# A gated up projection by Strassen's block product for 38 of 44 column pairs, with the up and the down projection as two phases

## The chip, the cores and the metric

The kernel runs on one core of a Trainium2 chip. The metric is device time in microseconds of one execution. The kernel before takes 2750.92 us, the median of three runs (2749.88 to 2751.28).

## The reference

One layer of a hybrid encoder block for 16 meta tokens followed by 512 tokens of width 2048, in float32. What bears on the change is its second half:

```
r = r + rmsnorm(mixer(rmsnorm(r)))
h = rmsnorm(r, ffn_pre_g)                       # 2048 features
a = causal_dwconv(h @ w_up, conv_w, conv_b)     # 2048 -> 2 x 5632, width 3 along the tokens
gate, val = split(a, 2)
r = r + rmsnorm((gelu_tanh(gate) * val) @ w_down, ffn_post_g)   # 5632 -> 2048
return r[:, 16:]
```

The mixer ahead of it (forgetting attention and multi-scale pools, their gates, then W_out) ends in 16 feature tiles `m` of 128 features, which W_out multiplies.

## The kernel before

Activations lie transposed, 128 features by tokens; weights are the stationary operand of TensorE (PE). Each float32 product is carried as three: x_hi*w_hi, x_lo*w_hi, x_hi*w_lo, where hi is the value rounded to the float32r multiplier's 12 bits and lo = value - hi. So one 128x128 weight tile and one block of tokens take three matmuls. Past the mixer only 514 tokens count (two meta tokens, since the convolution looks two back), in two halves: 258 and 256 columns.

**Weights.** `order` lists chunks of 16 weight tiles. Each chunk moves in two halves of 128x1024 (`load_next`, L133, on SP's DMA queue, six buffers). `convert_next` makes hi by a copy on ScalarE (ACT, L146) and lo by a subtraction on VectorE (DVE, L147), into four buffers each. `weights` calls it one to two halves ahead of the matmuls that use them.

**Side work.** `Side` holds Python generators that emit work for ACT, DVE, POOL and SP between the matmuls. `tick` counts the matmuls' columns at 2330 columns per us; when the time that a generator yielded has run out, its next piece is emitted. Only the first generator of the list runs. `finish` emits all that is left at once. Every engine then executes its instructions in the order in which they were emitted, and waits at an instruction whose operands or buffer aren't ready.

**Order around the change.** W_out runs for 16 output tiles; some for both halves of the tokens, the others first for half 0 and then for half 1. Beside its last 12 steps (half 1) runs `mixer_norm` of half 0: residual, second RMSNorm, and hi and lo of h (L701 to L718). The norm's factor per token (`rs2`) is left out of h and multiplied in when the product of W_up leaves PSUM (L759, L774). Then the first five gate/value pairs of W_up run in halves (`up_half`): all ten tiles for half 0, beside `mixer_norm` of half 1, then all ten for half 1, beside `combine`. The other 39 pairs run whole (`up_full`, L770): 16 weight tiles x 3 x 2 halves = 96 matmuls for a gate tile and 96 for a value tile. `combine` (L738 to L746) does the convolution, the gelu and the product with the value, and splits the result into hi and lo.

W_up and W_down alternate: `up_group(g+1)` makes four pairs, `down` multiplies the four tiles of group g with W_down and adds to 16 accumulators in SBUF (L806, L808). The last group of W_down runs in two halves of the tokens with the last norm beside it (`final`).

SBUF holds 68 slots of 128x528 float32 for activations (`F`). PSUM has three tiles of two banks and two tiles of one bank.

Of the kernel before, what the change touches and what calls it, by code (L numbers as in the profile page):

```python
# [23 lines left out]
RAW, HI, LO = 6, 4, 4  # L24
NOUT = 6
# [11 lines left out]
HB = T0 + NA  # L37
H = 8
# [4 lines left out]
EPS = 1e-6  # L43
NEG = -1e30
# [16 lines left out]
def block(ctx, tc, xT, win, wf, wao, wpw, wpo, wout, wup, wdn, consts, out):  # L61
# [5 lines left out]
    fp = ctx.enter_context(tc.tile_pool(name="act", bufs=68))  # L67
    wp = ctx.enter_context(tc.tile_pool(name="wts", bufs=2))
    sp = ctx.enter_context(tc.tile_pool(name="small", bufs=4))
    pp = ctx.enter_context(tc.tile_pool(name="psum", bufs=2, space=PSUM))  # L70
# [8 lines left out]
    def s_ps(name):  # L79
        return pp.tile([P, 512], F32, name=name, tag="s", bufs=2)  # L80
# [25 lines left out]
    # W_out: some tiles for all tokens at once, the others for each half of the tokens  # L106
# [15 lines left out]
    # each chunk holds 16 tiles of [128, 128] and moves in two halves  # L122
    raws, ready = [], []
    at = {"load": 0, "conv": 0, "use": 0}
    NL = 2 * len(order)

    def load_next():
        n = at["load"]
        if n < NL:
            key = order[n // 2]  # L130
            raw = wp.tile([P, 1024], F32, name="wraw", tag="wraw", bufs=RAW)
            c = 1024 * (n % 2)
            nc.sync.dma_start(raw, srcs[key[0]](*key[1:])[:, c:c + 1024])  # L133
            raws.append(raw)
            at["load"] += 1

    def convert_next(copy=act.copy):
        n = at["conv"]
        if n < NL - 8:
            if n == at["load"]:  # L140
                load_next()
            raw = raws[n]
            raws[n] = None
# [4 lines left out]
            ready.append((hi, lo))  # L148
            at["conv"] += 1

    def weights(*key, ahead=1):
        """the next chunk, as a function from the tile's number to its hi and lo parts"""
# [3 lines left out]
        while at["conv"] < min(NL - 8, 2 * n + 2 + (2 if ahead else -1)):  # L156
            convert_next()
        while at["load"] < min(NL, 2 * n + 2 + 2 * ahead + RAW):
            load_next()
        def w(t):  # L160
            if t >= 8 and ahead:
                while at["conv"] < min(NL - 8, 2 * n + 5):
                    convert_next()
            c = P * (t % 8)
            hi, lo = ready[2 * n + t // 8]
            return hi[:, c:c + P], lo[:, c:c + P]
        return w

    def last_weights(i):
        """tile i of the last group of W_down, in slots of the activations"""  # L170
        at["quarter"] = at.get("quarter", 2 * NL - 2 * 4 * 2)
        while at["quarter"] < min(2 * NL, 2 * NL - 16 + i + 5):
            q = at["quarter"]
            raw = raws[q // 2][:, 512 * (q % 2):512 * (q % 2 + 1)]
# [4 lines left out]
            while at["load"] < min(NL, q // 2 + 1 + RAW):  # L179
                load_next()  # L180
# [5 lines left out]
    class Side:  # L186
        """generators, one after another, that emit work and yield how long (us of products) to wait"""
# [27 lines left out]
    def mm3(parts, nk, w, x):  # L215
        """parts: (psum slice, rhs slice); w(k), x(k) -> (hi, lo)."""
        us = sum(3 * (xs.stop - xs.start) / 2330.0 for _, xs in parts)
        for k in range(nk):
            wh, wl = w(k)
            xh, xl = x(k)  # L220
            for j, (a, b) in enumerate(((wh, xh), (wh, xl), (wl, xh))):
                for po, xs in parts:
                    pe.matmul(po, a, b[:, xs], start=k == 0 and j == 0, stop=k == nk - 1 and j == 2)  # L223
            side.tick(us)

# [6 lines left out]
    def rstd_from(accs, dst, n, ps=None):  # L232
        """dst = 1 / sqrt(sum over the partitions and accs / D + EPS), on every partition"""
# [97 lines left out]
    def forget():  # L331
        """c = cumsum(logsigmoid(f))"""
# [88 lines left out]
    def attention(h, r):  # L421
# [5 lines left out]
        # values: [keys, head dim]  # L427
# [11 lines left out]
        # scores of the two meta queries the convolution reaches back to  # L439
# [35 lines left out]
        # P^T: [keys, queries]  # L475
# [83 lines left out]
    def half_proj(name, w, i, xs_h, xs_l):  # L559
        """an M-tile of a product with K = 1024; weights hold two M-tiles."""  # L560
# [3 lines left out]

    mp, sig = [], {}
    for i in range(16 + LAG):
        if i < 16:
            sig[i] = gate("pga", 32 + i)
        if i >= LAG:
# [8 lines left out]
            mp.append(m)  # L578

# [39 lines left out]
    HALF = [(0, NA, T0), (NA, NB, HB)]  # L619
    mh, ml = [None] * KT, [None] * KT  # L620

    def split_m(e, ks):
        o, n, c = HALF[e]
        for k in ks:
            if e == 0:
                mh[k], ml[k] = F("mh", F32R), F("ml", F32R)
            split(mp[k][:, c:c + n], mh[k][:, c:c + n], ml[k][:, c:c + n])

    for i in range(16 + LAG2):
        if i < 16:  # L630
# [14 lines left out]
        if i >= 16:  # L645
            split_m(0, range(14) if i == 16 else (14, 15))

# [7 lines left out]
    r_dram = dp.tile([KT, P, SEQ], F32, name="r_dram")  # L655
    hb = [[], []]
    rs2 = rstd[:, T0:]
# [4 lines left out]
    def mixer_out(i, es):  # L662
        w = weights("out", i)
        if len(es) == 2:
            big = mm_ps("pw2")
            pss = [big[:, 254:512], big[:, 512:768]]
        else:
            pss = [s_ps("pw")[:, :HALF[es[0]][1]]]
        mm3([(ps, slice(HALF[e][2], HALF[e][2] + HALF[e][1])) for e, ps in zip(es, pss)], KT, w,
            lambda k: (mh[k], ml[k]))  # L670
        for e, ps in zip(es, pss):
            n = HALF[e][1]
            t = mix[e][i] = F("mix", n=NA)
            act.copy(t[:, :n], ps)
            sq = F("sq2", n=NA)
            act.activation(sq[:, :n], ps, AF.Square)  # L676
            if macc[e] is None:
                macc[e] = sq
            else:
                dve.tensor_tensor(macc[e][:, :n], macc[e][:, :n], sq[:, :n], op=OP.add)  # L680

    def mixer_norm(e, mix, acc, pace):
        o, n, c = HALF[e]
        yield 4.0
        rs1, acc2 = F("rs1", n=NA), F("acc3", n=NA)
        xs = [None] * (KT + 3)

        def x_load(i):
            if i < KT:
                xs[i] = F("x2", n=NA)  # L690
                nc.sync.dma_start(xs[i][:, :n], xT[i][:, c:c + n])
# [3 lines left out]
        rstd_from([acc], rs1[:, :n], n)  # L695
        rows = []
        for i in range(KT + 2):
            yield pace
            if i < KT:
                t = mix[i]  # L700
                dve.scalar_tensor_tensor(t[:, :n], t[:, :n], col(C_G[1] + i), rs1[:, :n], op0=OP.mult, op1=OP.mult)  # L701
            if i >= 2:
                p, hl, g, sq = rows[i - 2]
                dve.scalar_tensor_tensor(hl[:, NA:NA + n], p[:, :n], g, f32(hl[:, :n]), op0=OP.mult, op1=OP.subtract)
                if i > 2:
                    pool.tensor_tensor(acc2[:, :n], acc2[:, :n], sq[:, :n], op=OP.add)
                rows[i - 2] = None
            if i < KT:
                pool.tensor_tensor(t[:, :n], t[:, :n], xs[i][:, :n], op=OP.add)
                xs[i] = None  # L710
                x_load(i + 3)
                rows.append((t, F("h2", F32R, 516), col(C_G[2] + i), F("sq3", n=NA) if i else acc2))
                s = max(c, META)
                nc.sync.dma_start(r_dram[i][:, s - META:c + n - META], t[:, s - c:n])
            if 1 <= i <= KT:
                p, hl, g, sq = rows[i - 1]
                act.activation(hl[:, :n], p[:, :n], AF.Identity, scale=g)
                act.activation(sq[:, :n], p[:, :n], AF.Square)  # L718
                hb[e].append(hl)
        yield 3.0  # L720
        rstd_from([acc2], rs2[:, o:o + n], n)
# [10 lines left out]
    yacc = [None] * KT  # L732

    def combine(zg, zv, f, acts):
# [16 lines left out]
        yield 0.1  # L751

    def up_half(e, m, z):
        o, n, c = HALF[e]
        w = weights("up", m)
        ps = s_ps("pu0")
        mm3([(ps[:, :n], slice(0, n))], KT, w,
            lambda k: (hb[e][k][:, :n], hb[e][k][:, NA:NA + n]))
        dve.tensor_tensor(z[:, o:o + n], ps[:, :n], rs2[:, o:o + n], op=OP.mult)  # L759

    def up_full(m):
        w = weights("up", m)
        ps = mm_ps("pup")
# [180 lines left out]
```

## Time and profile before

| what | value |
|---|---|
| time, median of 3 runs | 2750.92 us (2749.88 to 2751.28) |
| profiled execution, span from the first to the last instruction | 2750.2 us |
| PE busy | 2701.5 us, 98% of the span, 20581 matmuls |
| DVE busy | 1332.0 us, 48% |
| ACT busy | 872.1 us, 32% |
| POOL busy | 146.1 us, 5% |
| mean granted TensorE clock | 0.993 of full |
| moved by DMA | 289.87 MB, mean 105 GB/s |

The page gives the span of the profiled execution and no other time for it; it lies 0.7 us below the median of the runs. Busy shares are means over stages that differ. Matmuls are pipelined (one lasts about 0.28 us while the next starts 0.12 us after it), so that PE's rate is read from the distances between starts.

### The profile page before, as it was taken

The numbers are of one execution on the slowest core, as the hardware profiler recorded it, in microseconds if no ns is written. First come the engines' busy times: TensorE is split into PE (matmuls) and PEld (weight loads), VectorE is DVE, ScalarE is ACT, GpSimd is POOL, SyncE is SP. The second block draws the span as 40 slices with busy tenths as digits, with TensorE's granted clock in tenths as the row PEclk, the third lists the DMA queues.
The fourth block names the chain that finished last, engine by engine and source line by source line (L and its number), as shares of the span: only waits on it lengthen the run. The fifth ranks groups of instructions, "written<-read, shape, count | busy, mean of one in ns | idle before, by whom it ended". The sixth has DMA issues, their size and how long they took to land. (4 is left out here: it accounts for less than half of the span.)

```text
span 2750.2 us, 47156 instructions
## 1 busy us (share of the span) xinstructions
PE 2701.5 (98%) x20581; PEld 2604.2 (95%) x20581; DVE 1332.0 (48%) x1762; ACT 872.1 (32%) x1214; POOL 146.1 (5%) x176
## 2 busy tenths in 40 slices
PE   8999999999999999999999999999999999999996
PEld 7999999999999999999989898989898989898985
DVE  7655543223533344687633545353535444444447
ACT  4433342222322233555432222222222222222223
POOL 3000000000000000143000000000000000000003
PEclk9999999999999999999999999999999999999998
DMA  4322222222222224676422222222222222222223
GB/s 175 101 86 78 74 81 95 95 94 88 92 92 93 93 92 131 200 223 209 142 94 93 92 93 94 95 96 93 92 93 96 93 96 92 93 92 94 91 77 123
DMA packets 93967, 289.87 MB, mean 105 GB/s; under 512 B 10294, under 2 KB 26936, under 8 KB 93760
## 3 DMA queue, kind: packets, MB, share of 16 engines
q1 hardware_dynamic: 93056, 284.68, 31.0%
q8 instruction: 161, 2.64, 0.4%
q0 software_dynamic: 704, 2.18, 0.3%
q14 instruction: 46, 0.38, 0.0%
HBM read 278.41 MB, written 8.41 MB: 104 GB/s over the span
## 5 line engine op out<-in xcount | busy, mean ns | idle before, releaser
L147 DVE TENSOR_TENSOR wlo<-wraw,whi 128x1024 fp32r<-128x1024 f32 x494 | 613.9, 1245 | 581.8 <-ACT whi L146 578.0
L146 ACT CAST whi<-wraw 128x1024 fp32r<-128x1024 f32 x494 | 516.3, 1048 | 1174.3 <-PE pup L770 445.8
L770 PE MATMUL pup<-h,whi 128*128 128x258 f32 (+1 forms) x4992 | 794.5, 281 | 0.0
L770 PEld LDWEIGHTS pup<-h,whi 128*128 128x128 f32 x4992 | 681.3, 189 | 0.8
L770 PE MATMUL pup<-h,wlo 128*128 128x258 f32 x2496 | 501.1, 282 | 0.0
L770 PEld LDWEIGHTS pup<-h,wlo 128*128 128x128 f32 x2496 | 382.5, 189 | 0.0
L774 DVE TENSOR_TENSOR z<-pup,rstd 128x514 f32<-128x514 f32 x78 | 54.1, 694 | 262.6 <-PE pup L770 262.6
L223 PE MATMUL pw<-mh,whi 128*128 128x258 f32 (+1 forms) x512 | 135.0, 284 | 3.8 <-ACT sq L676 3.7
L223 PE MATMUL pw<-mh,wlo 128*128 128x258 f32 (+1 forms) x512 | 134.6, 283 | 0.0
L223 PE MATMUL pw<-ml,whi 128*128 128x258 f32 (+1 forms) x512 | 134.4, 283 | 0.0
L223 PE MATMUL pdm<-fl,whi 128*128 128x512 f32 x320 | 126.1, 394 | 0.0
L223 PE MATMUL pdm<-fh,wlo 128*128 128x512 f32 x320 | 126.0, 394 | 0.0
L223 PE MATMUL pd<-fh,whi 128*128 128x512 f32 x320 | 125.9, 393 | 0.0
L223 PE MATMUL pdm<-fh,whi 128*128 128x512 f32 x320 | 125.9, 393 | 0.0
L223 PE MATMUL pd<-fl,whi 128*128 128x512 f32 x320 | 125.7, 393 | 0.0
L223 PE MATMUL pd<-fh,wlo 128*128 128x512 f32 x320 | 125.7, 393 | 0.0
L223 PE MATMUL pu<-h,whi 128*128 128x258 f32 (+1 forms) x640 | 118.5, 288 | 1.8 <-DVE z L759 1.8
L808 DVE TENSOR_TENSOR yacc<-yacc,pd 128x512 f32<-128x512 f32 x72 | 49.5, 687 | 125.4 <-PE pd L223 125.4
L223 PEld LDWEIGHTS pu<-h,whi 128*128 128x128 f32 x640 | 101.1, 194 | 2.1 <-issue 2.0
L223 PE MATMUL pga<-xh,whi 128*128 128x258 f32 (+1 forms) x512 | 102.8, 282 | 0.0
L223 PE MATMUL pgp<-xh,wlo 128*128 128x258 f32 (+1 forms) x512 | 102.5, 282 | 0.0
L223 PE MATMUL pga<-xh,wlo 128*128 128x258 f32 (+1 forms) x512 | 102.4, 281 | 0.0
(294 smaller groups left out, 4857.8 us busy)
## 6 DMA issues: line engine op xcount, KB each, us to landing
wraw<-wup SPq DMA_DIRECT2D x196, 512.0 KB, 3.5
wraw<-win SPq DMA_DIRECT2D x128, 512.0 KB, 3.5
wraw<-wdn SPq DMA_DIRECT2D x88, 512.0 KB, 3.4
wraw<-wout SPq DMA_DIRECT2D x56, 512.0 KB, 3.6
wraw<-wao SPq DMA_DIRECT2D x16, 512.0 KB, 3.4
wraw<-wpo SPq DMA_DIRECT2D x16, 512.0 KB, 3.6
xr<-xT SPq DMA_DIRECT2D x16, 264.0 KB, 6.2
r_dram<-mix SPq DMA_DIRECT2D x32, 128.0 KB, 2.8
```

Of the source, the lines that this page charges most:

```text
L146: copy(hi, raw)
L147: dve.tensor_tensor(lo, raw, f32(hi), op=OP.subtract)
L223: pe.matmul(po, a, b[:, xs], start=k == 0 and j == 0, stop=k == nk - 1 and j == 2)
L770: pe.matmul(ps[:, 254 + o:254 + o + n], a, hb[e][k][:, b:b + n], start=k == 0 and j == 0, stop=k == KT - 1 and j == 2)
L774: dve.tensor_tensor(z[:, :NT], ps[:, 254:768], rs2, op=OP.mult)
L808: dve.tensor_tensor(yacc[i], yacc[i], ps, op=OP.add)
```

## The change

It takes the same result by another order of sums. For 38 of the 44 pairs, W_up's two tiles (gate, value) by its two halves of the input features form a 2x2 block matrix A, and h by feature halves and token halves a 2x2 block matrix B. Instead of eight block products the kernel takes seven (Winograd's form of Strassen's product): A11*B11, A12*B21, S2*T2, S1*T1, S3*T3, A22*B22 and S4*T4, where S1 = A21+A22, S2 = S1-A11, S3 = A11-A21, S4 = A12-S2, and T1 to T4 are such sums of blocks of h. Each block product is 8 weight tiles x 3 matmuls of 258 columns; both token halves have 258 columns and share two.

- The weight stream is now a list of loads and a list of conversions (`units`). A pair loads four halves and converts seven; the four sums of weights are made by DVE in `unit_source`. `pair_weights` converts three units ahead (LOOK).
- `up_pair` runs the seven products into three PSUM banks a, b, c. Some add onto a bank that already holds a product (`more`), after a copy of it (`snap`, ACT) has been taken for another output. Three sums on DVE and one copy on ACT make the gate and the value.
- The sums of h need the finished norm: `mixer_norm` now makes two passes per half, first residual and squares, then h with its factor, its hi and lo, and a copy of h to DRAM. `sums_of_h` loads the copies and makes T1 to T4 with hi and lo, beside the second half of the pairs in halves, of which there are now six; there `combine` is put ahead of it in the list.
- All of W_up runs before W_down. `combine` writes the gated tile to DRAM (GpSimd's DMA queue); `act_group` loads four tiles and splits them.
- There are 62 slots in place of 68. Ten of the mixer's 16 tiles `m` go through DRAM between its stages (`mp_store`, `mp_load`). From the FFN on PSUM is eight tiles of one bank. `final` loads the residual in smaller steps.

```diff
-    NH = 5
+    NH = 6
     ups = lambda f0, f1: [("up", s * FT + f) for f in range(f0, f1) for s in (0, 1)]
     order += ups(0, NH) * 2
-    for g in range(NG):
-        if g + 1 < NG:
-            order += ups(max(NH, (g + 1) * GRP), (g + 2) * GRP)
-        order += [("dn", g, m) for m in range(4)]
+    order += [("pair", f) for f in range(NH, FT)]
+    order += [("dn", g, m) for g in range(NG) for m in range(4)]
...
+            units += [(i, at0) for i in ("11", "12", "S2", "S1", "S3", "S4", "22")]
...
+        if kind == "S3":
+            def done():
+                drop(n + 2)
+                dve.tensor_tensor(a12, a12, sums["s2"], op=OP.subtract)
+            return a21, done
+        if kind == "S4":
+            return a12, lambda: drop(n + 1)
+        if kind == "S1":
+            def done():
+                dve.tensor_tensor(a21, a11, a21, op=OP.subtract)
+                drop(n)
+            return sums["s1"], done
...
+        dve.tensor_tensor(s1, a21, a22, op=OP.add)
+        dve.tensor_tensor(s2, s1, a11, op=OP.subtract)
+        return s2, lambda: None
...
+        def unit(i):
+            prepare(u + i + 1 + LOOK)
+            load_ahead()
...
-    def mixer_norm(e, mix, acc, pace):
+    def mixer_norm(e, mix, acc, pace, pace2):
...
+            if i > 2:
+                (dve if i % 2 else pool).tensor_tensor(acc2, acc2, sqs[i - 2], op=OP.add)
...
+        yield 2.0
+        rstd_from([acc2], rs2, n)
+        for i in range(KT + 1):
+            yield pace2
+            if i:
+                hl = hb[e][i - 1]
+                dve.tensor_tensor(hl[:, NA:], mix[i - 1], f32(hl[:, :NA]), op=OP.subtract)
+            if i < KT:
+                t = mix[i]
+                dve.scalar_tensor_tensor(t, t, col(C_G[2] + i), rs2, op0=OP.mult, op1=OP.mult)
+                hl = F("h2", F32R, 2 * NA)
+                act.copy(hl[:, :NA], t)
+                nc.sync.dma_start(h_dram[e, i], t)
                 hb[e].append(hl)
...
-            side.add(mixer_norm(0, mix[0], macc[0], 2.7))
+            side.add(mixer_norm(0, mix[0], macc[0], 2.2, 2.0))
     side.finish()
-    side.add(mixer_norm(1, mix[1], macc[1], 2.1))
+    side.add(mixer_norm(1, mix[1], macc[1], 1.8, 1.5))
...
+    def sums_of_h():
+
+        for k in range(HK):
+            t13, t24 = F("t13", n=2 * NA), F("t24", n=2 * NA)
+            for t, parts in ((t13, ((0, k), (1, k))), (t24, ((1, HK + k), (0, HK + k)))):
+                for j, (e, i) in enumerate(parts):
+                    nc.sync.dma_start(t[:, NA * j:NA * (j + 1)], h_dram[e, i])
+            yield 4.0
+            b11, b12, b22, b21 = t13[:, :NA], t13[:, NA:], t24[:, :NA], t24[:, NA:]
+            dve.tensor_tensor(b11, b12, b11, op=OP.subtract)
+            dve.tensor_tensor(b12, b22, b12, op=OP.subtract)
+            h13, l13 = F("h13", F32R, 2 * NA), F("l13", F32R, 2 * NA)
+            act.copy(h13, t13)
+            dve.tensor_tensor(b22, b22, b11, op=OP.subtract)
+            dve.tensor_tensor(b21, b21, b22, op=OP.subtract)
+            h24, l24 = F("h24", F32R, 2 * NA), F("l24", F32R, 2 * NA)
+            act.copy(h24, t24)
+            yield 1.5
+            dve.tensor_tensor(l13, t13, f32(h13), op=OP.subtract)
+            dve.tensor_tensor(l24, t24, f32(h24), op=OP.subtract)
...
+            yield 1.5
...
-        yield 1.5
+        yield 2.2
         for z, a, m in ms:
             dve.scalar_tensor_tensor(a, z[:, 1:NT - 1], col(C_W + 88 + m), a, op0=OP.mult, op1=OP.add)
-        for z, a, m in ms:
             dve.scalar_tensor_tensor(a, z[:, 0:SEQ], col(C_W + m), a, op0=OP.mult, op1=OP.add)
+            yield 2.8
         act.activation(g, g, AF.Gelu_apprx_tanh)
-        yield 2.0
+        yield 2.8
         dve.tensor_tensor(g, g, v, op=OP.mult)
-        yield 0.7
-        hi, lo = F("fh", F32R, SEQ), F("fl", F32R, SEQ)
-        split(g, hi, lo)
-        acts.append((hi, lo))
+        nc.gpsimd.dma_start(act_dram[f], g)
...
+        product(0, a, "11")
+        p1 = snap(a)
+        product(1, b, "21")
+        if late:
+            side.add(late)
+        product(2, a, "T2", True)
+        dve.tensor_tensor(zg[:, :NA], p1, b, op=OP.add)
+        u2 = snap(a)
+        product(3, c, "T1")
+        p5 = snap(c)
+        product(4, a, "T3", True)
+        product(5, c, "22", True)
+        dve.tensor_tensor(zv[:, NA:NT], p5[:, 2:], a[:, 2:], op=OP.add)
+        product(6, a, "T4", True)
+        dve.tensor_tensor(zg[:, NA:NT], u2[:, 2:], c[:, 2:], op=OP.add)
+        act.copy(zv[:, :NA], a)
+        side.add(combine(zg, zv, f))
...
             side.finish()
+            side.add(sums_of_h())
...
-                side.add(combine(zs.pop(f), zs.pop(FT + f), f, acts[f // GRP]))
+                done = combine(zs.pop(f), zs.pop(FT + f), f)
+                side.gens.insert(0, done) if side.gens else side.add(done)
+    side.finish()
...
+    for f in range(NH, FT):
+        up_pair(f, act_group(0) if f == FT - 1 else None)
```

## Rows read from the trace of the kernel before

**Rows 1.** The page: span, and busy time of each engine.
```profile
span 2750.2 us, 47156 instructions
...
PE 2701.5 (98%) x20581; PEld 2604.2 (95%) x20581; DVE 1332.0 (48%) x1762; ACT 872.1 (32%) x1214; POOL 146.1 (5%) x176
```

**Rows 2.** Waits of PE, whole span: total us, times, longest.
```profile
PE pw L223 <- ACT sq L676: 3.7, 2, 2.4
PE ps_rs L241 <- DVE z L759: 2.8, 1, 2.8
PE pu L223 <- DVE z L759: 1.8, 1, 1.8
```

**Rows 3.** Timeline, whole pairs of W_up: start, duration, engine, line, operation.
```profile
1602.10 1.05 ACT L146 CAST whi<-wraw 128x1024 fp32r<-128x1024 f32 x1 [4.66 <-PE pup L770]
...
1603.18 1.23 DVE L147 TENSOR_TENSOR wlo<-wraw,whi 128x1024 fp32r<-128x1024 f32 x1 [4.49 <-ACT whi L146]
...
1608.03 0.69 DVE L774 TENSOR_TENSOR z<-pup,rstd 128x514 f32<-128x514 f32 x1 [3.63 <-PE pup L770]
...
1619.44 0.69 DVE L774 TENSOR_TENSOR z<-pup,rstd 128x514 f32<-128x514 f32 x1 [3.03 <-PE pup L770]
```

**Rows 4.** Timeline of PE, pairs in halves: half 0, then half 1.
```profile
1212.15 0.41 PE L223 MATMUL pu<-h,whi 128*128 128x258 f32 x2
...
1216.12 0.41 PE L223 MATMUL pu<-h,whi 128*128 128x258 f32 x2
...
1283.81 0.40 PE L223 MATMUL pu<-h,whi 128*128 128x256 f32 x2
...
1289.15 0.40 PE L223 MATMUL pu<-h,whi 128*128 128x256 f32 x2
```

**Rows 5.** Groups by shape, DVE and ACT, 1500 to 1700 us, and (last) 1280 to 1337.
```profile
L147 DVE TENSOR_TENSOR wlo<-wraw,whi 128x1024 fp32r<-128x1024 f32 x36 | 44.1, 1225 | 36.8 <-ACT whi L146 36.5
L743 DVE SCALAR_TENSOR_TENSOR cv<-z,cs,cv 128x512 f32<-128x512 f32 x12 | 8.5, 748 | 0.0
...
L746 DVE TENSOR_TENSOR cv<-cv 128x512 f32<-128x512 f32 x7 | 4.8, 691 | 0.5
...
L146 ACT CAST whi<-wraw 128x1024 fp32r<-128x1024 f32 x36 | 37.8, 1050 | 128.3 <-PE pup L770 65.1 <-PE pd L223 36.2 <-issue 27.0
...
L759 DVE TENSOR_TENSOR z<-pu,rstd 128x256 f32<-128x256 f32 x10 | 4.2, 421 | 1.3 <-PE pu L223 1.3
```

**Rows 6.** Timeline of DVE, pairs in halves, half 1.
```profile
1299.72 0.42 DVE L759 TENSOR_TENSOR z<-pu,rstd 128x256 f32<-128x256 f32 x1
1300.06 2.36 DVE L147 TENSOR_TENSOR wlo<-wraw,whi 128x1024 fp32r<-128x1024 f32 x2
```

**Rows 7.** Timeline of PE: the waits between 1180 and 1260 us.
```profile
1184.79 0.39 PE L223 MATMUL pw<-mh,whi 128*128 128x256 f32 x1 [1.33 <-ACT sq L676]
...
1193.10 0.39 PE L223 MATMUL pw<-mh,whi 128*128 128x256 f32 x1 [2.39 <-ACT sq L676]
...
1255.21 0.48 PE L223 MATMUL pu<-h,whi 128*128 128x258 f32 x2 [1.83 <-DVE z L759]
```

**Rows 8.** Windows: length, busy us and counts by engine, PEclk, DMA share, GB/s.
```profile
1160.00:1180.00 20.00, 19.95 (x169) 19.75 (x168) 18.53 (x23) 12.40 (x24) 12.96 (x12) 1.00 0.80 256
1180.00:1200.00 20.00, 16.29 (x123) 15.88 (x122) 14.18 (x21) 10.81 (x23) 11.38 (x12) 0.91 0.59 190
...
1240.00:1260.00 20.00, 18.17 (x138) 17.99 (x137) 19.34 (x25) 11.48 (x21) 16.31 (x14) 0.91 0.74 231
...
1600.00:1800.00 200.00, 200.00 (x1504) 191.65 (x1503) 90.73 (x106) 54.84 (x63) 0.00 (x0) 1.00 0.28 94
```

**Rows 9.** Groups by shape, 1140 to 1280 us (both norms of h).
```profile
L147 DVE TENSOR_TENSOR wlo<-wraw,whi 128x1024 fp32r<-128x1024 f32 x44 | 62.5, 1422 | 12.7 <-ACT whi L146 12.1 <-DMA r_dram<-mix 0.5
```

**Rows 10.** Timeline of SP's queue and of POOL at 1148 us.
```profile
1148.40 0.37 SPq L691 DMA_DIRECT2D x<-xT  x1
...
1148.48 1.59 POOL L709 TENSOR_TENSOR mix<-mix,x 128x258 f32<-128x258 f32 x1 [746.82 <-DVE mix L701]
```

More of the change, by code (lines that the diff above doesn't have):

```diff
@@ L37 @@
 HB = T0 + NA
+H2 = L - NA
 H = 8
@@ L43 @@
 EPS = 1e-6
+NF = 62
+NSP = 10
 NEG = -1e30
@@ L121, in block @@
     }
-    raws, ready = [], []
-    at = {"load": 0, "conv": 0, "use": 0}
-    NL = 2 * len(order)
+    loads, units, base = [], [], []
+    for key in order:
+        base.append(len(units))
+        if key[0] == "pair":
+            at0 = len(loads)
+            for m in (key[1], FT + key[1]):
+                loads += [(wup[m], 0), (wup[m], 1024)]
+            units += [(i, at0) for i in ("11", "12", "S2", "S1", "S3", "S4", "22")]
+        else:
+            for c in (0, 1024):
+                units.append(("", len(loads)))
+                loads.append((srcs[key[0]](*key[1:]), c))
+    raws, ready, sums = {}, {}, {}
+    at = {"load": 0, "conv": 0, "use": 0, "live": 0}
+    NU = len(units)
+    NL = len(loads)
     def load_next():
@@ L129, in load_next, with raw_of, drop, load_ahead @@
         if n < NL:
[L130 removed]
+            src, c = loads[n]
             raw = wp.tile([P, 1024], F32, name="wraw", tag="wraw", bufs=RAW)
[L132 to L134 removed]
+            nc.sync.dma_start(raw, src[:, c:c + 1024])
+            raws[n] = raw
             at["load"] += 1
+            at["live"] += 1
+    def raw_of(n):
+        while at["load"] <= n:
+            load_next()
+        return raws.get(n)
+    def drop(n):
+        del raws[n]
+        at["live"] -= 1
+    def load_ahead():
+        while at["load"] < NL and at["live"] < RAW:
+            load_next()
+    def unit_source(kind, n):
+        if kind == "":
+            return raw_of(n), lambda: drop(n)
+        a11, a12, a21, a22 = (raw_of(n + i) for i in range(4))
+        if kind == "11":
+            return a11, lambda: None
+        if kind == "12":
+            return a12, lambda: None
+        if kind == "22":
+            return a22, lambda: drop(n + 3)
+        if kind == "S3":
[10 more added lines that the diff above has]
+            return sums["s1"], done
+        s1, s2 = (wp.tile([P, 1024], F32, name="wsum", tag="wsum", bufs=2) for _ in range(2))
+        sums.update(s1=s1, s2=s2)
+        dve.tensor_tensor(s1, a21, a22, op=OP.add)
+        dve.tensor_tensor(s2, s1, a11, op=OP.subtract)
+        return s2, lambda: None
     def convert_next(copy=act.copy):
         n = at["conv"]
[L139 to L143, printed above, removed]
+        if n < NU - 8:
+            kind, first = units[n]
+            raw, done = unit_source(kind, first)
             hi = wp.tile([P, 1024], F32R, name="whi", tag="whi", bufs=HI)
@@ L178, in last_weights @@
             at["quarter"] += 1
-            while at["load"] < min(NL, q // 2 + 1 + RAW):
-                load_next()
+            if q % 2:
+                drop(q // 2)
+            load_ahead()
         return last_w[i]
@@ L222, in mm3 @@
                 for po, xs in parts:
-                    pe.matmul(po, a, b[:, xs], start=k == 0 and j == 0, stop=k == nk - 1 and j == 2)
+                    pe.matmul(po, a, b[:, xs], start=k == 0 and j == 0 and not more,
+                              stop=k == nk - 1 and j == 2, skip_group_check=more)
             side.tick(us)
@@ L777, in block, with snap @@
-    acts = [[] for _ in range(NG)]
-    def up_group(g):
-        for f in range(max(NH, g * GRP), (g + 1) * GRP):
-            zg, zv = up_full(f), up_full(FT + f)
-            side.add(combine(zg, zv, f, acts[g]))
+        ps = s_ps("pu0")[:, :NA]
+        mm3([(ps, slice(0, NA))], KT, w, lambda k: h_block(e, k))
+        act.copy(z[:, NA * e:NT], ps[:, 2 * e:]) if e else act.copy(z[:, :NA], ps)
+    def snap(src):
+        t = sp.tile([P, NA], F32, name="snap", tag="snap", bufs=4)
+        act.copy(t, src)
+        return t
@@ new lines, in up_pair, with product @@
+    def up_pair(f, late=None):
+        unit = pair_weights(f)
+        a, b, c = (s_ps(n)[:, :NA] for n in ("pua", "pub", "puc"))
+        zg, zv = F("z"), F("z")
+        def product(i, ps, block, more=False):
+            mm3([(ps, slice(0, NA))], HK, unit(i), BLOCKS[block], more)
+        product(0, a, "11")
[15 more added lines that the diff above has]
+        side.add(combine(zg, zv, f))
```

192 lines of the change are left out of this document (114 added, 78 removed).

## The prediction

> **What bounds the kernel now.** I read the page first: PE is busy 98% of 2750.2 us, every other engine under half [rows 1]. Then PE's waits: nearly all of them lie between 1180 and 1270 us, at the norm that feeds W_up, and they are short [rows 2]. Elsewhere PE runs matmul after matmul, so the time is the number of matmuls times the distance between their starts. That distance I took from the timeline: two results of a W_up tile are read 1619.44 - 1608.03 = 11.41 us apart and 96 matmuls lie between, 0.1189 us each [rows 3]. In the windows DVE is at 45% in this stretch [rows 8]. What remains to be asked is whether the work that replaces matmuls fits on DVE, and in which places it comes too late.
>
> **1. Matmuls removed.** A whole pair costs 2 x 11.41 = 22.82 us [rows 3]. After, it has 7 x 8 x 3 = 168 matmuls of 258 columns. Their distance is bounded by the pairs in halves, where each weight tile also meets only one block of tokens: (1216.12 - 1212.15)/33 = 0.1203 for 258 columns beside a busy DVE, (1289.15 - 1283.81)/45 = 0.1187 for 256 [rows 4]. I take 0.1195: 20.08 us, a gain of 2.74 per pair and 38 x 2.74 = -104 us (-99 to -109). The sixth pair in halves has 192 matmuls as it had before: nothing.
>
> **2. DVE in a pair.** Seven lo's and four sums of 128x1024 (the sums are not in the trace; nearest is the lo, same shape and operation), four convolution steps, one product and three sums of 258 columns. By durations: 11 x 1.225 + 4 x 0.748 + 0.691 + 3 x 0.421 = 18.4 us [rows 5]. Back to back they start closer: two lo's together take 2.36, so 1.13 for the first, and a 256-column sum is followed after 0.34 [rows 6]; with 0.1 us off the other operations that is about 16.8. So DVE is at 84 to 92% of 20.08 us. The windows have both neighbours: at 18.53 of 20 us (93%) PE lost nothing, at 19.34 (97%) it had 18.17 [rows 8]. ACT has seven casts of 1.05 [rows 5], four copies and three activations, some 11 us. So the load fits; the order may not.
> The Trainium skill, "VectorE: DVE Perf Modes", section "Terms", says that the pipe is flushed after every DVE operation and the next one can't issue until it is empty. By it the sum would be the 18.4; the trace differs, as those starts lie 0.1 us closer than the durations. Neither reaches 20.08.
>
> **3. The wait inside a pair.** Product 6 adds onto bank a, which DVE must first have read for the value (`zv`). That sum stands in DVE's queue behind the lo of the unit three ahead, whose cast waits for product 4 to release its buffer. From the end of product 4: cast 1.05, lo 0.03 later and 1.23 long [rows 3], sum 0.42 [rows 5], together 2.73, with some 0.1 us for each of the hand-overs 2.8 to 3.2. Product 5 gives 24 x 0.1195 = 2.87 of cover. I take 0.25 us of waiting per pair, 38 x 0.25 = +10 us (0.05 to 0.65: +2 to +25). The copies of p1, u2 and p5 have a whole product between them and their use, and the combine of the pair before is emitted in products 0 to 3 by its yields: nothing. Behind the waiting DVE sum stand the next weight sums, three units early.
>
> **4. The sums of h, emitted at once.** Half 1 of the pairs in halves gives 12 x 16 ticks of 3 x 258/2330 = 0.332, that is 63.8 us of side time. `sums_of_h` needs 8 x 7 = 56 of it, but from 10.6 us on there is a combine ahead of it in the list, each yields 10.7 us, and a new one comes every 10.6. So `sums_of_h` finishes one k of eight, and each combine is overtaken before its last product. `finish` then emits the whole last combine, five left products and seven k's. DVE, counted from the end of the halves: 2.2 us for ACT's copy and steps, 4 x 0.7 + 0.7 of the last combine, 5 x 0.65 of products, so the sums start at about 8.5 us. Each k is four sums of 258 (0.4) and two lo's of 516 (0.69; the nearest row is the 512-column product) [rows 5], 3.0 us; seven end at 29.5. PE has products 0 and 1 to do (5.7 us), then needs T2 k by k, and would be through product 2 at 8.6; it is through at 29.9. That is 21 us, and product 3 waits 1.3 more for a lo emitted behind it all. A clock drop costs 1.8 more (step 5). I take +25 us. Below: 15, if DVE gets on with the combine sooner. Above: 45, if every load of h copies lands after a k is done (some 3 us each for seven); against that stands that the load of the fourth x tile was issued at 1148.48 - 1148.40 = 0.08 us before the first tile's reader had begun, so that slots are not taken in turn with their last reader [rows 10].
>
> **5. The two norms.** Before, PE loses 3.7 + 2.8 + 1.8 = 8.3 us there [rows 2], and its clock falls to half (1.2 GHz) after the longer waits: 2.39 and 1.83 us were followed by a window at 0.91, which is 20 x 0.09 = 1.8 us lost each; the wait of 1.33 alone was not [rows 7, 8]. Three such drops (the third after the 2.8) make the loss 13.7. DVE is slow there, 1.42 us for a lo beside POOL's additions [rows 9]. After, the first pass has half of POOL's sums and DVE no lo of h, but the norm of half 0 needs 4 + 18 x 2.2 + 2 + 17 x 2.0 = 79.6 us of side time and has 63.8: eight of its last steps are emitted at once, each a chain DVE, ACT, DVE of about 1.25 us, while PE takes 0.36 per k. That is 10.6 - 5.3 = 5 us of waiting plus a drop. The second norm just fits (63.9) with DVE nearly full: 5 more and a drop. Together about 14, against 13.7 saved: 0 (-10 to +15).
>
> **6. The rest.** Reloading ten tiles of `m` ahead of W_out starts about 9 us before their first use and keeps pace with W_out's first step within a us; at the change from up to down one split and a combine stand in DVE's queue: +1 each (0 to +5 and 0 to +4). W_down's phase alone loads DVE less than half. The end, with its loads in steps: 0.
>
> **Sum.** -104 + 10 + 25 + 0 + 2 = -67 on the profiled span of 2750.2; the median of the runs lies 0.7 above it, so 2684 us. All low ends together give 2649, all high ends 2746.
>
> **Rivals.**
> A. Everything new is covered (`sums_of_h` waits little, no wait in the pair): -104 + 4 = 2651. For it: DVE at 93% cost nothing once [rows 8]. Against: the yields in step 4 are arithmetic. Chance 0.12, with times to 2660.
> B. DVE becomes the bound in the pairs: it runs like the 97% window, where PE did 18.17 of 20 us [rows 8]. A pair then takes 20.08 x 20/18.17 = 22.1, the wait is +77 in place of 10: 2751 if all of it comes, 2712 if half of it does, about 2730 between them. It needs the operations of step 2 to cost 6% more than their durations. Nothing on POOL computes in that stretch, so the 1.42 us of [rows 9] should not come. Chance 0.13.
> C. The clock. Small waits where PSUM banks are cycled halve it again and again: one drop of 1.8 us in each of 38 pairs is +68, so 2752, no change. For it: the three drops. Against: none followed the 1.33 us wait [rows 7], five times what I expect in a pair. The Trainium skill, "TensorE: Matmul & The Clock Gate", section "A second HAM failure mode: psum-queue depth-cycling", reports such micro-idles making the clock oscillate; by that rule the time would be this one, and here the trace leans against it. Chance 0.03.
> D. Slower: DVE's idle time turns out to be latency. Each lo in the whole pairs is preceded by 36.8/36 = 1.02 us of waiting for its cast [rows 5]. If that stays with each of the seven lo's, a pair takes 18.4 + 7 x 1.02 = 25.5 on DVE, 2.7 over the 22.82 of now: +103, with step 4 about 2880. It decides from (22.82 - 18.4 - 25/38)/7 = 0.54 us per lo. Against it: two lo's ran with nothing between them [rows 6], since casts are done ahead when DVE is behind; the waiting now is DVE being early. Chance 0.05.
>
> **Chances.** Forecast 0.67 (its own range 2660 to 2710), A 0.12, B 0.13, C 0.03, D 0.05. The range 2655 to 2728 leaves out half of A, part of B, C and D. A measurement of this kernel can't tell less than 0.2% (5.5 us) from no change: faster is the forecast, A and nearly all of B, 0.92; same C and the rest of B, 0.03; slower D, 0.05.
>
> **What would show it.** About 19,670 matmuls (912 fewer); a pair 20.1 to 20.4 us apart; one wait of PE per pair, for a DVE `zv`; some 20 us in which PE gets a matmul group only every 3 us, right behind the halves, waiting for l24; clock at full through the pairs. Wrong: DVE above 95% in the pairs with PE waiting for `wlo` (B), repeated half clock (C), or the gap behind the halves missing (A).

## The result and the profile after

The changed kernel takes 2718.03 us, the median of four runs (2717.10 to 2719.34); the kernel before took 2751.10 beside it. The ratio is 0.9879, with a 95% interval of 0.9865 to 0.9893: 33 us faster where 67 were forecast. The time lies inside the range, but the gain is half of the forecast one.

The page of the kernel after, its totals and two lines of its 40 slices (to be read beside [rows 1]):

```profile
span 2715.4 us, 46577 instructions
...
PE 2622.0 (97%) x19669; PEld 2519.4 (93%) x19669; DVE 1652.6 (61%) x2144; ACT 1044.2 (38%) x1524; POOL 149.1 (5%) x204
...
PE   8999999999999999988969999999999999999995
...
PEclk9999999999999999998989999999999999999998
```

The 912 matmuls are gone and PE's busy time fell by 79.5 us, but the span only by 34.8. Each slice is 67.9 us; counted from 0, slices 17, 18 and 20 of PE fall to 8, 8 and 6 (1154 to 1290, and 1358 to 1426 us): the norms, and the start of the whole pairs.

To find where the rest went, I cut both traces at PE's first matmul of each stage. Before, W_up and W_down alternate, so there 38 whole pairs are put at 22.82 us each, and W_down is what remains:

| stage | before, us | after, us | difference |
|---|---|---|---|
| up to W_out | 1022.5 | 1022.3 | -0.2 |
| W_out, to the first matmul of W_up | 189.7 | 202.2 | +12.5 |
| six pairs in halves (before: five, and one whole at 22.82) | 146.8 | 165.2 | +18.4 |
| 38 whole pairs | 867.2 | 801.6 | -65.6 |
| W_down but its last group | 444.0 | 444.6 | +0.6 |
| the rest | 80.0 | 79.5 | -0.5 |

The pairs gave nearly what the forecast had for them (-104 + 10 + 25 = -69), in part by luck, since errors cancel there (steps 1, 3 and 4 below). The stretch of the two norms, W_out and the halves, was put at 0 and cost +30.9. That is nearly all of the error of 32.2 us (-34.8 in place of -67).

The waits of PE in that stretch of the kernel after, 1020 to 1440 us (total, times, longest), against the three rows of [rows 2]:

```profile
PE pua L310 <- ACT snap L914: 25.3, 1, 25.3
PE pu L310 <- ACT sq L787: 9.2, 1, 9.2
PE ps_rs L329 <- DVE acc L816: 5.8, 2, 3.9
PE pu L310 <- DVE wlo L215: 4.0, 6, 0.8
PE pu L310 <- DVE h L831: 1.4, 1, 1.4
PE pw L310 <- DVE ml L300: 1.4, 1, 1.4
PE pu L310 <- ACT whi L214: 1.3, 2, 0.8
PE pu L310 <- ACT h L836: 1.0, 3, 0.3
```

The first row is the gap behind the halves. The row for `ml` is W_out's first step, where `m` is reloaded (step 6 of the prediction). The others lie in the stretch of the norms; with the `ml` row they come to 24.1 us, against 8.3 before. That is 15.8 of the 30.9 us. The granted clock, 0.98 and 0.94 in the two stages of that stretch against 0.99 and 0.98 before, is worth up to 10 more, less what of it falls into the waits. And 1348 of its matmuls had 256 columns before and have 258 now: by the distances of [rows 4] 1348 x 0.0016 = 2.2 us, which the prediction left out. Windows of the kernel after (busy time of PE, PEld, DVE, ACT, POOL with counts, granted clock, DMA share, GB/s), to be read beside [rows 8]:

```profile
1200.00:1220.00 20.00, 15.37 (x128) 15.15 (x127) 11.82 (x20) 8.91 (x16) 0.00 (x0) 0.95 0.51 152
1220.00:1240.00 20.00, 14.57 (x81) 13.30 (x82) 13.87 (x26) 7.93 (x17) 0.00 (x0) 0.71 0.45 146
...
1400.00:1420.00 20.00, 0.00 (x0) 0.00 (x0) 18.70 (x39) 8.46 (x14) 0.00 (x0) 0.50 0.35 113
1600.00:1800.00 200.00, 200.00 (x1662) 200.00 (x1662) 172.38 (x189) 101.77 (x140) 5.41 (x10) 1.00 0.36 119
```

In the first two PE idles for a quarter of the time, yet DVE is busy for only 59 and 69% and ACT for 45 and 40%. No engine is the bound there; they wait for each other. In the third PE stands still and DVE is near its limit (94%; ACT 42%). In the steady pairs PE never stops, with DVE at 86% and the full clock.

**Why the norm's second pass is slow.** ACT in the kernel after, while PE is in W_out (start, duration, engine, line, operation, and in brackets the idle time before it and who ended it):

```profile
1198.90 0.41 ACT L836 CAST h<-mix 128x258 fp32r<-128x258 f32 x1 [3.75 <-DVE mix L834]
...
1202.83 0.41 ACT L836 CAST h<-mix 128x258 fp32r<-128x258 f32 x1 [2.03 <-DVE mix L834]
1203.15 1.04 ACT L214 CAST whi<-wraw 128x1024 fp32r<-128x1024 f32 x1
1206.22 0.41 ACT L836 CAST h<-mix 128x258 fp32r<-128x258 f32 x1 [2.03 <-DVE mix L834]
...
1223.50 0.41 ACT L836 CAST h<-mix 128x258 fp32r<-128x258 f32 x1 [0.89 <-DVE mix L834]
1223.81 0.37 ACT L785 COPY mix<-pw 128x258 f32<-128x258 f32 x1
1224.08 0.39 ACT L787 ACTIVATE sq<-pw 128x258 f32<-128x258 f32 x1
```

and DVE at the same time:

```profile
1204.22 1.23 DVE L215 TENSOR_TENSOR wlo<-wraw,whi 128x1024 fp32r<-128x1024 f32 x1 [1.43 <-ACT whi L214]
1205.37 0.42 DVE L831 TENSOR_TENSOR h<-mix,h 128x258 fp32r<-128x258 f32 x1
1205.70 0.48 DVE L834 SCALAR_TENSOR_TENSOR mix<-mix,cs,rs 128x258 f32<-128x258 f32 x1
```

One step of the pass multiplies on DVE (L834) and casts on ACT (L836) in the same turn. ACT's cast of h at 1206.22 waits for DVE's multiplication at 1205.70; that stands behind a weight's lo at 1204.22; that waits for the weight's cast at 1203.15; and that stands behind the cast of h at 1202.83. Each engine, in order, waits for the other: this is the lockstep. The casts of h come 3.4 to 3.9 us apart where a weight's cast lies between them, and 1.3 where none does. The eight paced steps from 1198.90 to 1223.50 take 24.6 us, 3.1 each, where side time allows 2.0; in the norm of half 1 the fifteen from 1284.49 to 1321.76 take 2.5 each, where it allows 1.5. ACT falls behind, and takes W_out's last result out of PSUM only at 1223.81, though PE had been through W_out 9.15 us before the first matmul of W_up, which started at 1224.52:

```profile
1224.52 0.80 PE L310 MATMUL pu<-h,whi 128*128 128x258 f32 x2 [9.15 <-ACT sq L787]
...
1232.71 0.85 PE L310 MATMUL pu<-h,whi 128*128 128x258 f32 x2 [0.33 <-ACT h L836]
1234.01 0.85 PE L310 MATMUL pu<-h,whi 128*128 128x258 f32 x2 [0.34 <-ACT h L836]
```

The last two show the steps that were emitted at once: 1234.01 - 1232.71 = 1.30 us per k, as the forecast had it (1.25).

**The gap behind the halves.** DVE, ACT and PE of the kernel after:

```profile
1394.78 3.70 DVE L902 TENSOR_TENSOR cv<-cv 128x512 f32<-128x512 f32 x6
1398.40 0.42 DVE L863 TENSOR_TENSOR t<-t 128x258 f32<-128x258 f32 x1
...
1401.50 0.42 DVE L863 TENSOR_TENSOR t<-t 128x258 f32<-128x258 f32 x1
...
1420.47 0.37 ACT L914 COPY snap<-pua 128x258 f32<-128x258 f32 x1
...
1420.89 0.58 PE L310 MATMUL pua<-h,whi 128*128 128x258 f32 x1 [25.28 <-ACT snap L914]
1421.27 0.42 PE L310 MATMUL pua<-l,whi 128*128 128x258 f32 x1
1421.48 0.42 PE L310 MATMUL pua<-h,wlo 128*128 128x258 f32 x1
```

Six left products, then rounds of the sums of h 1401.50 - 1398.40 = 3.10 us apart, as forecast. But PE didn't get product 2 k by k: it waited once, for the copy of product 0. That copy was issued behind all the casts of the rounds on ACT, and each of these waits for DVE's sums.

### The profile page after: what moved, and what is told of

Same layout as the page of the kernel before. It is cut to its first block, busy times and chain, and to the rows that moved or that the text cites. A ratio compares the mean times of both kernels' runs of the same rounds, so it can differ in the third digit from the quotient of the medians.

```text
span 2715.4 us, 46577 instructions
## 1 busy us (share of the span) xinstructions
PE 2622.0 (97%) x19669; PEld 2519.4 (93%) x19669; DVE 1652.6 (61%) x2144; ACT 1044.2 (38%) x1524; POOL 149.1 (5%) x204
## 4 chain that ended last, share of the span: by engine, by line
PE 89%; DVE 5%; issue 2%; ACT 2%; DMA 2%; POOL 0%; SPq 0%; DVEq 0%; ACTq 0%; POOLq 0%
PE pd L310 17%; PE pua L310 16%; PE puc L310 8%; PE pgp L310 7%; PE pga L310 7%; PE pw L310 6%; PE pu L310 6%; PE pub L310 4%; PE pv L310 3%; PE pao L310 3%; PE pk L310 3%; PE ppo L310 3%; PE pq L310 3%; ACT whi L214 1%; PE pa L589 1%
## 5 line engine op out<-in xcount | busy, mean ns | idle before, releaser
L310 PE MATMUL pua<-h,whi 128*128 128x258 f32 x1520 | 370.2, 284 | 28.5 <-ACT snap L914 25.3
L310 PE MATMUL pua<-h,wlo 128*128 128x258 f32 x1216 | 345.6, 284 | 0.0
L310 PEld LDWEIGHTS pua<-h,whi 128*128 128x128 f32 x1520 | 267.6, 190 | 28.9 <-ACT snap L914 25.5
L310 PE MATMUL pua<-l,whi 128*128 128x258 f32 x912 | 259.1, 284 | 0.0
L310 PEld LDWEIGHTS pua<-h,wlo 128*128 128x128 f32 x1216 | 231.9, 191 | 0.0
L310 PE MATMUL puc<-h,whi 128*128 128x258 f32 x912 | 198.7, 284 | 0.0
L310 PEld LDWEIGHTS pua<-l,whi 128*128 128x128 f32 x912 | 173.8, 191 | 0.0
L310 PE MATMUL puc<-h,wlo 128*128 128x258 f32 x608 | 172.4, 284 | 0.0
L310 PE MATMUL pu<-h,whi 128*128 128x258 f32 x768 | 149.9, 296 | 13.1 <-ACT sq L787 9.2
L310 PEld LDWEIGHTS puc<-h,whi 128*128 128x128 f32 x912 | 152.9, 190 | 0.0
```

The lines of the kernel that those rows point to most:

```text
L310: pe.matmul(po, a, b[:, xs], start=k == 0 and j == 0 and not more, stop=k == nk - 1 and j == 2, skip_group_check=more)
```

## The experiments

The kernel before, run beside each of them, took 2750.83 to 2751.27 us, so their times can be compared with each other. Two theories at first. L (lockstep): the norm's second pass is slow because ACT and DVE wait for each other in each step. P (PSUM): the halves now draw on a pool of eight banks that opens where W_out's tiles end, so that the first matmul of W_up waits for W_out's last reader.

**x1: the second pass staggered.** The multiplication of step i, the cast of step i - 1 and the subtraction of step i - 2 are emitted together, so that none needs what was issued just ahead of it.

```diff
-        for i in range(KT + 1):
+        for i in range(KT + 2):
             yield pace2
-            if i:
-                hl = hb[e][i - 1]
-                dve.tensor_tensor(hl[:, NA:], mix[i - 1], f32(hl[:, :NA]), op=OP.subtract)
+            if i >= 2:
+                hl = hb[e][i - 2]
+                dve.tensor_tensor(hl[:, NA:], mix[i - 2], f32(hl[:, :NA]), op=OP.subtract)
+            if 1 <= i <= KT:
+                hl = F("h2", F32R, 2 * NA)
+                act.copy(hl[:, :NA], mix[i - 1])
...
```

> The changed kernel, with the second pass of the norm staggered: the multiply by the norm's factor in one step, the cast to hi in the next, the subtraction of hi in the one after (before: multiply and cast in the same step). Theory L (in the second pass ScalarE and VectorE wait for each other in turn, since each h cast waits for a multiply that stands behind a weight lo which waits for a weight cast behind the h cast before): the steps of 3.3 to 4 us fall to the 2.0 of their yields, the 9.2 us wait at the start of the halves shrinks below 4, time 2718 to about 2700 (12 to 25 less). Rival P (the first W_up matmul waits since the new PSUM pool takes the bank that W_out's last square still reads) and rival W (too much VectorE work in the stretch, whatever its order): within 4 us of 2718.

2695.07 us (2693.93 to 2698.16), ratio to before 0.9797 [0.9782, 0.9812]: 23 us below the changed kernel. ACT in the same stretch of this kernel, with two casts of h 2.3 us apart and no wait for DVE between them (two of the first nine still wait, 1.72 us each):

```profile
1198.72 1.05 ACT L214 CAST whi<-wraw 128x1024 fp32r<-128x1024 f32 x1
1199.66 0.42 ACT L834 CAST h<-mix 128x258 fp32r<-128x258 f32 x1
1200.98 1.05 ACT L214 CAST whi<-wraw 128x1024 fp32r<-128x1024 f32 x1 [0.91 <-ACT h L834]
1201.94 0.41 ACT L834 CAST h<-mix 128x258 fp32r<-128x258 f32 x1
```

The first W_up matmul starts at 1216.60 after a wait of 1.20 instead of 9.15, and the halves take 153.9 us instead of 165.2. Of the 30.9 us that the stretch had cost, 19.2 are gone in the trace (which is of the slowest of the four executions, 2698.16 us), and the windows of 1200 to 1240 show the full clock again. The operations are the same and only their order differs, so rival W, too much work on DVE, is out for these 23 us.

**x2: PSUM as before while the halves run**; the pool of eight banks opens behind them.

```diff
-    psum.close()
-    banks[:] = psum.enter_context(tc.tile_pool(name="psum2", bufs=8, space=PSUM)), 8
...
-        ps = s_ps("pu0")[:, :NA]
+        ps = (s_ps if len(halves) % 2 else mm_ps)("pu0")[:, :NA]
...
+    psum.close()
+    banks[:] = psum.enter_context(tc.tile_pool(name="psum2", bufs=8, space=PSUM)), 8
```

> The changed kernel, with the old PSUM tiles (three of two banks and two of one, taken in turn) kept until the pairs in halves are done, and the eight one-bank tiles from there on. Rival P: the 9.2 us wait goes, with the clock drop behind it 11 less, about 2707. Theory L: the wait passes to h itself, which isn't ready; 0 to 4 less.

2717.92 us, ratio to before 0.9879 [0.9865, 0.9894]: no change. The 9.2 us wait went into 2.1 for `sq` and 4.9 for h itself. P falls: the banks only decided at which matmul PE noticed that h was late.

**x4: the other way round, the two-pass norm put into the kernel before**, with nothing of Strassen (h with its factor, its copies to DRAM, six pairs in halves, and W_up's results in halves read by copies on ACT).

> The kernel before, with only the norm's part of the change: two passes with the factor in h, copies of h written to DRAM (read by nobody), the same yields, six pairs in halves, W_up's results read by copies. If the norm's new order carries the loss that step 5 missed (theory L or W): 25 to 38 us above before, 2776 to 2789. If the loss comes from what stands beside it (new PSUM pool, fewer slots, the m tiles through DRAM): under 12 above.

2778.53 us (2778.24 to 2780.70), ratio to before 1.0100 [1.0085, 1.0115]: 27 us slower. Its first whole pair starts at 1382.52; in the kernel before that pair would come at 1336.18 + 22.82 = 1359.0, so 23.5 of the 28.4 us between the two profiled spans lie in this stretch. The casts of h are in lockstep here too:

```profile
1201.95 0.41 ACT L727 CAST h<-mix 128x258 fp32r<-128x258 f32 x1 [2.03 <-DVE mix L725]
...
1205.88 0.41 ACT L727 CAST h<-mix 128x258 fp32r<-128x258 f32 x1 [2.03 <-DVE mix L725]
```

So the loss comes with the norm's new form and the little that x4 takes over beside it; the sums of weights, the new PSUM pool and the new weight stream aren't needed for it. That the order within the pass makes it is what x1 shows.

**x7: x1 with the second norm's factor 4 us later** (`yield 6.0` for `yield 2.0`), against the remaining wait of 3.9 us for `acc`.

> x1_pipe with 6 in place of 2 us of yield ahead of the second norm factor, whose matmul waited 1.9 and 3.9 us for VectorE's sum of squares, each time with a clock drop behind it. If these waits are time on the path: 4 to 8 less than x1_pipe, 2687 to 2691. If the four us only move the end of the second pass back, so that the halves wait for h in their place: 2693 to 2699.

2694.34 us, 0.9796 [0.9781, 0.9810], 0.7 below x1, which is within what can be told from no change. In the trace both waits for `acc` (5.8 us) are gone, a wait of 0.9 for h came up, those for `wlo` grew by 0.7, and the stretch is 344.0 us long against 348.3; the profiled spans differ by 2.0. The time is in the second range, but h took over little of the wait, so whether these waits were on the path isn't settled.

**x3: shorter yields in the combines of the halves, the last combine behind the sums of h**, so that fewer rounds are left when the halves end.

```diff
-                done = combine(zs.pop(f), zs.pop(FT + f), f)
-                side.gens.insert(0, done) if side.gens else side.add(done)
+                done = combine(zs.pop(f), zs.pop(FT + f), f, (1.2, 1.2, 1.2, 1.0))
+                side.gens.insert(0, done) if side.gens and f < NH - 1 else side.add(done)
```

> The changed kernel, with shorter yields of combine beside the pairs in halves (4.7 us in all, before 10.7) and the last combine put behind sums_of_h: by the yields five to six of eight k's of the sums are emitted before the halves end. If the 25.3 us wait at product 2 of the first pair is VectorE's work emitted at once behind the halves, as step 4 of the prediction has it: the wait falls to 3 to 8 us, time 2698 to 2702. If it is the loads of the copies of h landing late: the wait stays above 15, time above 2708.

2709.36 us (2707.60 to 2710.30), 0.9846 [0.9830, 0.9862]: 8.7 below the changed kernel, half of what I expected. The wait for `snap` fell from 25.3 to 14.3 only: three rounds and the last combine were still emitted ahead of the copy. The wait at the first W_up matmul was 10.7, which isn't this edit's doing (x6 has 10.6).

**x5: x1 and x3, and what is left is emitted behind product 1 of the first pair**, that is behind the copy of product 0. (One round still came out beside product 0 by its yields, ahead of that copy.)

> x1_pipe and x3_sums together, and what is left of the side work is emitted behind product 1 of the first whole pair in place of ahead of product 0, so that the copy of p1 stands ahead of it in ScalarE's queue. In x3_sums three rounds of the sums of h (3.1 us each) and the last combine were left, and the wait at product 2 (14.3 us) ended with that copy. If the queue order makes the wait: PE meets T2 after some 4 to 6 us, time 2695 - 9 (as x3_sums) - 8 = 2676 to 2681. If the sums themselves are the limit: the wait stays above 10 under another name, 2684 to 2688.

2690.28 us (2688.68 to 2692.57), 0.9781 [0.9765, 0.9798]: 4.8 below x1, where I expected 14 to 19, and above the second range too. PE in this kernel, behind products 0 and 1:

```profile
1383.04 0.58 PE L310 MATMUL pua<-h,whi 128*128 128x258 f32 x1 [5.45 <-ACT snap L915]
...
1393.27 0.58 PE L310 MATMUL pua<-h,whi 128*128 128x258 f32 x1 [5.99 <-ACT h L871]
...
1396.39 0.58 PE L310 MATMUL pua<-h,whi 128*128 128x258 f32 x1 [1.58 <-ACT h L871]
```

The gap is now in three pieces, 13.0 us in all, and PE runs at half clock between them (0.54 in 1380 to 1400). Between the rounds stand the pair's own weight sums on DVE, and a load of copies of h that SP issued behind weight loads:

```profile
1387.42 1.22 DVE L191 TENSOR_TENSOR wraw<-wraw,wsum 128x1024 f32<-128x1024 f32 x1
1387.53 0.34 SPq L159 DMA_DIRECT2D wraw<-wup  x1
1387.92 2.46 SPq L861 DMA_DIRECT2D t<-h_dram  x4
1390.48 0.43 DVE L864 TENSOR_TENSOR t<-t 128x258 f32<-128x258 f32 x1 [1.85 <-DMA t<-h_dram]
```

**x8: x5 with x7's later factor and shorter yields for the sums of h** (9.0 once, then 2.5, 1.0, 1.0 for 4.0, 1.5, 1.5), and **x9: the same with those loads on POOL's queue.**

> Takes the staggered second pass, the later factor of the norm and the emission behind product 1, and gives the sums of h shorter yields (2.5, 1.0, 1.0 in place of 4.0, 1.5, 1.5; 9.0 ahead of the first, whose load DVE had to wait for). Side time of half 1 is 63.8 us; 9.0 and five combines of 4.6 leave 31.8, which is seven rounds of 4.5, so at most one round is left for the first pair. Theory (PE's gap behind the halves is the emission of rounds in one piece, whoever PE is seen to wait for): the waits of PE in front of product 2, 13.0 us with the emission behind product 1, fall under 4 and the half clock behind them goes; with 0.7 from the later factor the median is 2675 to 2681, against 2690. Rival (DVE in half 1 has no room: per pair in halves two lo's 2.5, one combine 3.7, 1.3 rounds of 3.1 = 10.2 of 10.6 us): the gap goes but PE waits for wlo and whi in half 1 grow by 8 us and more, and the median stays within 2686 to 2694.

> As the run before it, and the loads of the copies of h for the sums go through the POOL queue in place of SP's, where they stood behind weight loads that wait for a buffer. Theory (in the pair, the round waits for its load, 1.85 us on DVE and up to 6.0 on PE, because of that queue): 1 to 4 us below the kernel beside it if any round is still emitted in the pair; equal to it (within 2 us) if none is. Rival (the POOL queue's DMAs take longer to start): PE's or DVE's waits for t get longer, and the time is 2 us and more above it.

x8: 2686.95 us (2685.99 to 2689.45), 0.9769 [0.9752, 0.9785], the fastest of all, 64 below before. But it falls in the rival's range, though the rival's signs (no gap, and waits that grow by 8 us) didn't come either: PE still waited 12.1 us in front of product 2, and its waits for `whi` and `wlo` were 8.0 us in all, against 5.1 in x5. x9: 2691.28 us, 0.9782 [0.9768, 0.9797], 4.3 slower than x8: the rival of that run held. In it DVE waited 10.6 us for those loads (6.9 in x8), and the waits for `whi` came to 8.1.

**x6: the changed kernel without the four sums of weights.**

> The changed kernel without the four sums of weights (the raw blocks stand in for S1 to S4, so that the result is another): VectorE falls from 86% to about 63% of a pair. PE took 0.1203 us per matmul in the pairs of the changed kernel, against 0.1189 in the whole pairs before. If VectorE's traffic in SBUF makes the difference: 0.1190 to 0.1195, a pair at 20.0 to 20.1 us, time some 5 lower. If 258 columns in a row of single blocks make it: 0.1200 or more, time within 2 of 2718, which also says that the sums cost nothing.

2717.26 us, one run of a kernel that leaves these sums out. The window of the steady pairs, to be read beside the last one of the kernel after:

```profile
1600.00:1800.00 200.00, 200.00 (x1664) 200.00 (x1663) 128.08 (x149) 103.34 (x139) 5.42 (x10) 1.00 0.36 119
```

DVE falls from 86 to 64% and PE runs 1664 matmuls in place of 1662. So the sums of weights cost PE nothing that one run can show, and the distance of 200/1662 = 0.1203 us isn't their doing.

## Why the prediction was wrong

**1. Matmuls removed: right, 5 us too much.** 19669 matmuls, as forecast. From one pair to the next, by DVE's last sum of each:

```profile
1702.44 0.41 DVE L940 TENSOR_TENSOR z<-snap,puc 128x256 f32<-128x256 f32 x1
...
1722.66 0.42 DVE L940 TENSOR_TENSOR z<-snap,puc 128x256 f32<-128x256 f32 x1
```

A pair takes 1722.66 - 1702.44 = 20.22 us, and 38 x (22.82 - 20.22) = -98.8 in place of -104. I had taken 0.1195 us, between 0.1203 (258 columns) and 0.1187 (256) of [rows 4]; all of these matmuls have 258, so the first row alone was the one to use.

**2. DVE in a pair: right.** 86% in the pairs or 17.4 us of 20.22, inside the 84 to 92% (the closer sum, 16.8, comes to 16.6 by the terms that it names). The rule that the Trainium skill gives ("VectorE: DVE Perf Modes", section "Terms"), that the next operation waits for an empty pipe, would put 18.4 us or 91% there; the trace is nearer to the rows by which starts lie closer than the durations.

**3. The wait inside a pair: absent.** Forecast +10. Product 5 is S4*B22 and product 6 A22*T4 in the kernel (in the section on the change their factors are crossed). In the steady pair the sum that frees bank a ends just before product 6:

```profile
1715.18 0.40 PE L310 MATMUL puc<-h,whi 128*128 128x258 f32 x2
...
1717.52 0.41 DVE L938 TENSOR_TENSOR z<-snap,pua 128x256 f32<-128x256 f32 x1
...
1718.10 0.29 PE L310 MATMUL pua<-h,whi 128*128 128x258 f32 x1
```

1718.10 - 1717.93 = 0.17 us to spare. From the start of product 5 at 1715.18 the path to that sum's end takes 2.75 us, where the forecast had 2.8 to 3.2, and product 5 covers 2.92, where it had 2.87. So each was off by 0.1 us or so, and the wait of 0.25 put into the sum falls away. Only the last pair shows the wait, 3.2 us once, where `act_group`'s splits are on DVE too.

**4. The sums of h, emitted at once: right in size, wrong in its last link.** +25 forecast; 25.3 of waiting and 2.6 lost behind it at half clock. The sums start 1398.40 - 1389.7 = 8.7 us behind the halves (forecast 8.5, though the terms named there add up to 8.95). The count of seven rounds and 3.0 us each held (3.10). But PE waited for ACT's copy of product 0, behind the casts, not for `l24` k by k. It mattered for the cure: with four rounds fewer (x3) the gap shrank by 11.0 us and not by 12.4, and with the rest behind the copy (x5) by only 1.3 more.

**5. The two norms: the step that failed.** Forecast 0 (-10 to +15), measured +30.9 (+12.5 ahead of the first W_up matmul, +18.4 in the halves). I counted the second pass as side time: 17 steps at a yield of 2.0, with eight left over at 1.25 each. The eight left over came as said (1.30). What I had put at nothing is how long one paced step takes when its multiplication, its cast and its subtraction are strung between the weights' cast and lo on the same two engines: 3.1 us in place of 2.0 in half 0, and 2.5 in place of 1.5 in half 1, so that the second norm, which was to "just fit", came late too. This is shown from both sides: x1 takes the lockstep away and gives back 23 us, x4 puts the two passes into the kernel before and costs 27.

About 12 us of the stretch remain in x1's trace. There 4.6 are waits of PE (12.9 us against 8.3, with 1.4 for `ml` at W_out's start, which belongs to step 6) and 2.2 are the columns of half 1 (256 before, 258 now). The rest stays open. The two waits for `acc` may be part of it: in x7's trace, without them, 7.5 us remain (344.0 against 336.5). DVE's additional passes over h in the norm are another candidate, and no run took them away.

**6. The rest: right.** +0.6 and -0.5 in the down phase and the end, and the 1.4 of `ml` that is counted in step 5, against +2.

Put together: steps 1, 3 and 4 make -65.6 in place of -69. That is so close by luck: the matmuls gave 5 us less, the gap cost 3 more and the last pair's wait 3.2, some 2 us have no name, and the missing wait of 10 makes up for most of this. Step 6 is 2 less than forecast, and step 5 is the rest: -67 + 3.4 - 2.1 + 30.9 = -34.8, the difference of the profiled spans.

**The rivals.** A (all covered) and D (slower) are out. B (DVE the bound) is out: PE lost nothing at 86%. C (the clock) is out for the pairs: three banks are cycled in 38 pairs at a granted clock of 1.00. The Trainium skill, "TensorE: Matmul & The Clock Gate", section "A second HAM failure mode: psum-queue depth-cycling", reports an oscillating clock in such cycling; in these pairs PE had no idle time that the trace shows, so its condition wasn't met. The clock did fall where PE waited (0.71 and 0.50 in the windows above), but not by the length of a wait alone, as the last section shows.

**What stays open.** The gap in front of product 2 was never closed (25.3, 14.3, then 12 to 13 us). In x5 and x8 the trace shows rounds behind weight sums on DVE and behind loads on SP; POOL's queue for these loads (x9) made it no better. An order in which the copy of product 0 comes ahead of every round, and the rounds ahead of the pair's weight sums, wasn't tried.

## What to carry to other kernels

A paced generator says when work is issued, not how long a step takes: where one step hands a value from DVE to ACT and back, and other work does the same on these two engines, follow one step through both queues in order before you trust its yield. Emit such chains staggered, so that no instruction needs one issued just ahead of it on another engine; here that alone was worth 23 us, two thirds of what the whole change had gained. When two rows of the trace give a duration for two shapes, take the row of your shape, not the mean.

## What the runs showed of the hardware

- The distance of matmuls of 258 columns stayed at 200/1664 = 0.1202 us with DVE at 64% busy and 200/1662 = 0.1203 at 86%.
- After the 25.3 us wait the matmuls started 0.21 us apart (1421.27, 1421.48) instead of 0.12: the granted clock was at its lower level of 1.2 GHz when work came back. The windows of 5 us from 1420 and from 1425 have 0.50 and 0.89, so the gap cost 4.11 x 0.50 + 5 x 0.11 = 2.6 us more than its length:

```profile
1420.00:1425.00 5.00, 4.11 (x19) 4.11 (x20) 3.64 (x4) 1.88 (x3) 0.00 (x0) 0.50 0.18 51
1425.00:1430.00 5.00, 5.00 (x39) 5.00 (x39) 3.83 (x5) 2.98 (x5) 0.00 (x0) 0.89 0.55 174
```

- The same wait for the first norm's sum of squares, 1.91 to 1.94 us at 1193 to 1195, was followed by a lower clock in some traces and not in others: the window of 1180 to 1200 has 0.91 in the kernel after and in x1, and 1.00 in x2 and x5. So the prediction's price of 1.8 us for each longer wait isn't due every time.
- The loads of the copies of h landed 4.3 us after their issue from POOL's queue and 4.0 from SP's (medians of 32 each, x9 and x8): the queue change bought nothing.
